# Batched matmul minus a tensor: the identity built on VectorE, and the first row tile cut as one block of 128 rows

## The chip, the cores and the metric

One Trainium2 chip, one of its cores. Times are device microseconds. Below 2% a difference counts as "same".

## The reference

```python
batch, m, k, n = 16, 512, 1024, 768          # all float32
out = np.matmul(x, weight) - sub_value        # x: (16, 512, 1024), weight: (1024, 768)
```

The 16 x 512 rows are taken as 8192 rows, in 64 tiles of 128 ("m tiles"). 25.2 MB of sub_value, 33.6 of x and 3.1 of weight come in, 25.2 MB go out.

## The kernel before

A row of m tiles is loaded as one transfer. `S = 8` says how rows are dealt: in a segment of 1024 rows, partition p holds the eight rows 8p to 8p+7, and tile j is the j-th row of every partition. So a transfer of eight tiles moves one piece of 32 KB (x) or 24 KB (sub_value, out) per partition, while tile 0 alone is 128 rows of 4 KB that lie 32 KB apart.

```python
S = 8
TRANSFERS = [('x', 0, 1), ('w', 0, 1), ('x', 1, 1), ('w', 1, 1), ('x', 2, 1), ('w', 2, 1),
    ('x', 3, 2), ('w', 3, 1), ('s', 0, 1), ('x', 5, 3), ('s', 1, 3), ('x', 8, 4), ...
    ('x', 24, 8), ('o', 0, 8), ('s', 24, 8), ('x', 32, 8), ...          # cut
    ('o', 56, 5), ('o', 61, 2), ('o', 63, 1)]                           # (kind, first tile, tiles)
x_s = x_flat.rearrange("(s p j) k -> s p j k", p=P, j=S)                # the same for sub_value and out
...
pool.add(lambda: nc.gpsimd.memset(idle_w, 0.0), then=count("idle"))     # operands of the warm-up matmuls
pool.add(lambda: nc.gpsimd.memset(idle_x, 0.0), then=count("idle"))
pool.add(lambda: nc.gpsimd.memset(ident, 0.0), then=count("ident"))
pool.add(lambda: nc.gpsimd.affine_select(out=ident, ..., fill=1.0), waits=[(counter["ident"], 1)], ...)
```

All transfers go out from SyncE's queue in the order of the list, each as soon as its buffer allows. ScalarE casts x to fp16, TensorE (for some tiles VectorE) transposes it with the identity, TensorE multiplies, VectorE subtracts in place and SyncE stores. TensorE starts with 14 idle matmuls. Before any work, TensorE, ScalarE and VectorE make a first pass over a branch:

```python
nc.regs_mov(turn, 0); nc.br("turn_head", ...)
# turn_head: turn == 0 -> "past", else -> "work";  past: turn += 1, back to turn_head while turn < 2
with nc.body("work", ...):
    act.emit(act.ops); dve.emit(dve.ops[:NEAR]); ...    # TensorE: a head, a loop of 10, a tail
```

## Time and profile before

| | before |
|---|---|
| time, median of 3 (range) | 210.98 us (210.87 to 211.11) |
| profiled span | 209.0 us |
| bytes moved, mean rate | 87.08 MB, 417 GB/s |
| TensorE busy / VectorE busy | 94% / 61% |
| x tile 0 landed, first and last DMA engine | 3.95 / 5.99 us |
| last matmul starts / last store landed | 201.75 / 207.75 us |

The lines that carry the argument are quoted in the prediction. One reading aid: a transfer is split over 16 DMA engines, and the trace holds one landing event per engine. A transfer is complete with the last of the 16: the cast of x tile 0 starts at 6.01 us, just after the last landing at 5.99. I quote the first, the 13th and the last in order of time (the records don't name the engine), since in this program one to three engines trail the rest, or the mean of the 16. Such landings, packet durations and the moments of single instructions are worked out from the trace's own records; the profile's tables don't print them.

### The profile page before, as it was taken

What the parts mean: (1) busy time and instruction counts of PE and PEld (TensorE: products, weight loads), DVE (VectorE), ACT (ScalarE), POOL (GpSimd) and SP (SyncE); (2) the same over time, 40 slices, a digit from 0 to 9 for tenths busy, and PEclk for the clock granted to TensorE, in tenths of its full rate; (3) what the DMA queues carried; (4) which work ended last, traced back from release to release, by engine and by line L of the source; (5) the groups of instructions that cost most, each with busy time, mean ns of one, the idle gap of its engine ahead of it and who ended that gap; (6) DMA issues with size and microseconds to landing.
All of it is one profiled execution on the core that took longest, in us unless ns stands there. A gap on an engine that the chain in (4) does not pass through costs nothing.

```text
span 209.0 us, 2630 instructions
## 1 busy us (share of the span) xinstructions
PE 196.5 (94%) x1234; PEld 75.5 (36%) x700; DVE 127.0 (61%) x216; ACT 109.0 (52%) x113; POOL 1.4 (1%) x9
## 2 busy tenths in 40 slices
PE   6998799979999999999999999999999999999960
PEld 0133334324434433433443443344344244334410
DVE  0132153975994795598299379569839938952330
ACT  2555559615772761945645576193564737507300
POOL 2000000000000000000000000000000000000000
PEclk9999999999999999999999999999999999999996
DMA  6999999999999999999999999999999999999993
GB/s 196 411 429 427 432 424 438 436 415 439 437 439 433 420 423 442 445 426 425 447 426 419 447 419 423 456 439 415 440 436 411 430 437 437 419 433 442 414 411 125
DMA packets 5476, 87.08 MB, mean 417 GB/s; under 512 B 608, under 2 KB 608, under 8 KB 1888
## 3 DMA queue, kind: packets, MB, share of 16 engines
q1 hardware_dynamic: 5472, 87.03, 97.7%
q14 instruction: 3, 0.02, 0.1%
q8 instruction: 1, 0.02, 0.0%
HBM read 61.87 MB, written 25.17 MB: 416 GB/s over the span
## 4 chain that ended last, share of the span: by engine, by line
PE 75%; DMA 12%; DVE 6%; SPq 3%; issue 1%; DVEq 0%
PE po_b L184 67%; DMA so_ring<-in_sub_value_dram 12%; PE pt_b L321 8%; DVE xtp_b L354 3%; DVE so_ring L403 2%; SPq L284 2%; SPq L248 1%; SPq L554 0%; DVEq L60 0%; SPq L134 0%
## 5 line engine op out<-in xcount | busy, mean ns | idle before, releaser
L184 PE MATMUL po_b<-w_sb,xt_b 128*128 128x384 f16 x704 | 126.0, 326 | 0.7 <-DVE w_sb L251 0.7
L403 DVE TENSOR_TENSOR so_ring<-po_b,so_ring 128x768 f32<-128x768 f32 x64 | 60.8, 957 | 58.2 <-PE po_b L184 40.9
L334 ACT COPY xt_b<-pt_b 128x1024 f16<-128x1024 f16 x44 | 44.5, 1012 | 67.2 <-PE pt_b L321 66.3
L354 DVE STREAM_TRANSPOSE xtp_b<-x16p_b 32x256 f32<-32x256 f32 x144 | 62.7, 435 | 2.4 <-ACT x16p_b L303 0.2
L184 PE MATMUL po_b<-w_sb,xtp_b 128*128 128x384 f16 x320 | 61.3, 326 | 1.2 <-DVE xtp_b L354 1.1
L383 PEld LDWEIGHTS <-xt_b 128*128 128x128 f16 x352 | 34.4, 98 | 58.4 <-issue 55.1
L303 ACT CAST x_b<-x_ring 128x1024 f16<-128x1024 f32 x46 | 47.2, 1048 | 4.5 <-DMA x_ring<-in_x_dram 4.5
L321 PE MATMUL pt_b<-ident,x_b 128*128 128x128 f32 x184 | 47.5, 274 | 1.6 <-ACT x_b L303 1.5
L321 PEld LDWEIGHTS pt_b<-ident,x_b 128*128 128x128 f32 x184 | 25.4, 141 | 45.8 <-issue 36.3
L303 ACT CAST x16p_b<-x_ring 128x1024 f16<-128x1024 f32 x18 | 18.8, 1046 | 13.0 <-DMA x_ring<-in_x_dram 13.0
L383 PEld LDWEIGHTS <-xtp_b 128*128 128x128 f16 x160 | 15.7, 98 | 19.8 <-issue 17.7
L251 DVE CAST w_sb<-so_ring 128x768 f16<-128x768 f32 x8 | 4.1, 557 | 15.5 <-DMA so_ring<-in_weight_dram 15.5
L184 PE MATMUL po_b<-idle_x,idle_w 128*128 128x512 f16 x26 | 9.0, 503 | 2.1 <-POOL idle_x L171 2.1
L334 ACT COPY xtp_b<-pt_b 128x1024 f16<-128x1024 f16 x2 | 2.0, 1012 | 2.5 <-PE pt_b L321 2.5
L303 ACT ACT_TABLE_LOAD x1 | 1.3, 1283 | 1.8 <-issue 1.8
L413 PEld LDWEIGHTS <-idle_w 128*128 128x128 f16 x4 | 0.4, 100 | 2.0 <-POOL idle_x L171 2.0
L171 POOL MEMSET idle_x<- 128x512 f16 x1 | 0.5, 530 | 0.0
L485 ACT CAST stub<-ident 128x1 f16<-128x1 f32 x2 | 0.4, 194 | 0.0
L173 POOL TENSOR_SCALAR_AFFINE_SELECT ident<-ident 128x128 f32<-128x128 f32 x1 | 0.3, 294 | 0.1
L462 POOL MEMSET mark<- 128x1 f32 x1 | 0.1, 99 | 24.6 <-ACT xtp_b L334 24.6
L170 POOL MEMSET idle_w<- 128x128 f16 x1 | 0.2, 205 | 0.5 <-SPq L134 0.5
L172 POOL MEMSET ident<- 128x128 f32 x1 | 0.2, 205 | 0.0
(4 smaller groups left out, 0.4 us busy)
## 6 DMA issues: line engine op xcount, KB each, us to landing
so_ring<-in_sub_value_dram SPq DMA_DIRECT2D x7, 3072.0 KB, 24.3
out_dram<-so_ring SPq DMA_DIRECT2D x7, 3072.0 KB, 25.9
x_ring<-in_x_dram SPq DMA_DIRECT2D x5, 4096.0 KB, 22.8
x_ring<-in_x_dram SPq DMA_DIRECT2D x2, 2048.0 KB, 26.5
so_ring<-in_weight_dram SPq DMA_DIRECT2D x4, 768.0 KB, 8.8
x_ring<-in_x_dram SPq DMA_DIRECT2D x1, 3072.0 KB, 28.0
x_ring<-in_x_dram SPq DMA_DIRECT2D x2, 1024.0 KB, 24.4
out_dram<-so_ring SPq DMA_DIRECT2D x1, 1920.0 KB, 10.2
```

Of the source, the lines that this page charges most:

```text
L171: pool.add(lambda: nc.gpsimd.memset(idle_x, 0.0), then=count("idle"))
L184: return nc.tensor.add_instruction(mybir.InstMatmult(name=nc.get_next_instruction_name(), engine=full.engine, ins=list(full.ins), outs=lis ...
L248: sp.add(lambda st=st, at=at: nc.sync.dma_start(out=st, in_=w_c[at]), then=(sem, 16))
L251: lambda at=at, r=r, st=st: nc.vector.tensor_copy(out=w_sb[:, at, r], in_=st[:, r]),
L284: sp.add(lambda here=here, there=there: nc.sync.dma_start(out=here, in_=there), waits, (sem, 16))
L303: act.add(lambda: nc.scalar.copy(out=to, in_=x_in), waits, count("cast"))
L321: pe.add(lambda: nc.tensor.transpose(words, from_, ident), waits, count("turn") if last else None)
L334: act.add(lambda: nc.scalar.copy(out=to, in_=pt_b[:, b]), waits, count("evac"))
L354: dve.add(lambda: nc.vector.transpose(xt[b * Q : (b + 1) * Q, :, a * Q : (a + 1) * Q], x16[a * Q : (a + 1) * Q, :, b * Q : (b + 1) * Q],), ...
L383: pe.add(lambda weights=weights: nc.tensor.ldweights(weights, tile_position=(0, 0)), [w for w in waits if w[0] in ready])
L403: dve.add(lambda: nc.vector.tensor_tensor(out=o, in0=po[:, :, :NS], in1=o, op=mybir.AluOpType.subtract), [landed["s", mi], (counter["mul"] ...
L413: pe.add(lambda: nc.tensor.ldweights(idle_w, tile_position=(0, 0)), [(counter["idle"], 2)])
```

## The change

Its intent: make tile 0 one compact block, so that the first load starts well, and build the identity on an engine that idles at the start. Its core:

```diff
-S = 8
+SEGMENTS = [(0, 1), (1, 7)] + [(at, 8) for at in range(8, 64, 8)]
-    ('x', 24, 8), ('o', 0, 8), ('s', 24, 8), ...
+    ('x', 24, 8), ('o', 0, 1), ('o', 1, 7), ('s', 24, 8), ...
+    def view(flat, at, n):
+        first, size = next(one for one in SEGMENTS if one[0] <= at < sum(one))
+        rows = flat[first * P : (first + size) * P].rearrange("(p j) c -> p j c", p=P, j=size)
+        return rows[:, at - first : at - first + n]
-    pool.add(lambda: nc.gpsimd.memset(ident, 0.0), then=count("ident"))
-    pool.add(lambda: nc.gpsimd.affine_select(out=ident, ...), ...)
+    dve.add(lambda: nc.vector.memset(ones, 1.0), then=count("ident"))           # 128x32
+    dve.add(lambda: nc.vector.memset(ident, 0.0), then=count("ident"))
+    dve.add(lambda: nc.vector.tensor_tensor_scan(out=along, data0=ones, data1=ones, ...), ...)
+    dve.add(lambda: nc.vector.transpose(across, along), ...)
+    for a in range(P // Q):                                                     # four 32x32 blocks
+        dve.add(lambda here=here: nc.vector.tensor_tensor(out=ident[here, here],
+            in0=along[here], in1=across[here], op=mybir.AluOpType.is_equal), ...)
```

## The prediction

> **What bounds the kernel now.** I read the page's slices first, then the chain that ended last, then the waits of TensorE, then busy time by stretch, then the first microseconds in order of time.
>
> The slices and the DMA summary come first:
>
> ```profile
> PE   6998799979999999999999999999999999999960
> DMA  6999999999999999999999999999999999999993
> GB/s 196 411 429 427 432 424 438 436 415 439 437 439 433 420 423 442 445 426 425 447 426 419 447 419 423 456 439 415 440 436 411 430 437 437 419 433 442 414 411 125
> ...
> q1 hardware_dynamic: 5472, 87.03, 97.7%
> ```
>
> Each digit is a fortieth of the 209.0 us span. The reader is to see that the DMA engines are full from the second slice to the last but one, at 410 to 456 GB/s, and that TensorE is full as well. The data queue alone holds the 16 engines for 97.7% of the span. So there are two bounds that nearly touch, and the question is which of them sets the end, and where there is air.
>
> ```profile
> by line: PE po_b L184 67.3%; DMA so_ring<-in_sub_value_dram 12.4%; PE pt_b L321 7.5%; DVE xtp_b L354 3.3%; DVE so_ring L403 2.2%; SPq L284 2.2%; SPq L248 1.3%; issue 0.6%; SPq L554 0.0%; DVEq L60 0.0%; SPq L134 0.0%
> ...
> 8.72 25.85 DMA so_ring<-in_sub_value_dram
> 34.66 1.82 DVE so_ring L403 x2
> 39.08 0.96 DVE so_ring L403
> 42.77 0.96 DVE so_ring L403
> 45.79 0.81 PE po_b L184 x4
> ```
>
> This is the chain of waits in order of time (start, length, what). Up to 34.57 us it is one load of sub_value, then VectorE, and from 45.79 us TensorE and nothing else until 202.1. The waits of TensorE say the same:
>
> ```profile
> PE pt_b L321 <- ACT x_b L303: 1.5, 1, 1.5
> PE po_b L184 <- DVE xtp_b L354: 1.1, 1, 1.1
> PE po_b L184 <- DVE w_sb L251: 0.7, 2, 0.5
> ```
>
> Everything TensorE waits for lies in the first 46 us, and all three go back to a landing (x, sub_value, weight). Busy time by stretch (columns: PE, PEld, DVE, ACT, POOL, clock, DMA share, GB/s):
>
> ```profile
> 2.00:3.00 1.00, 0.95 (x3) 0.10 (x1) 0.00 (x0) 1.00 (x1) 0.12 (x1) 1.00 0.91 168
> 3.00:4.00 1.00, 1.00 (x4) 0.00 (x0) 0.00 (x0) 0.06 (x1) 0.00 (x0) 1.00 1.01 383
> 4.00:6.00 2.00, 2.00 (x6) 0.00 (x0) 0.00 (x0) 0.00 (x0) 0.00 (x0) 1.00 0.98 382
> 46.00:100.00 54.00, 54.00 (x351) 21.71 (x201) 39.80 (x68) 30.12 (x31) 0.00 (x0) 1.00 1.01 433
> ```
>
> TensorE is busy 54.00 of 54 us in the middle, and the engines move 433 GB/s. From 2 to 6 us the engines are occupied but move less: that is the only stretch before the end where bytes are lost. Last, the start of the work:
>
> ```profile
> 1.82 0.29 POOL L173 TENSOR_SCALAR_AFFINE_SELECT ident<-ident 128x128 f32<-128x128 f32 x1
> 2.05 5.90 PE L184 MATMUL po_b<-idle_x,idle_w 128*128 128x512 f16 x14 [2.05 <-POOL idle_x L171]
> 6.01 1.05 ACT L303 CAST x_b<-x_ring 128x1024 f16<-128x1024 f32 x1 [2.95 <-DMA x_ring<-in_x_dram]
> 7.79 0.60 PE L321 MATMUL pt_b<-ident,x_b 128*128 128x128 f32 x4
> 7.90 1.03 DVE L251 CAST w_sb<-so_ring 128x768 f16<-128x768 f32 x2 [7.90 <-DMA so_ring<-in_weight_dram]
> ```
>
> The identity was ready at 2.1 us and first used at 7.6. x tile 0 was cast by 7.06, but TensorE was still in its 14 warm-up matmuls, so it began the transposes half a microsecond later.
>
> One thing the page doesn't show, from the trace's landing events (16 per transfer, one per DMA engine): x tile 0 landed at 3.95 us on the first engine and at 5.99 on the last; weight piece 1 at 9.13 and 11.02; sub_value tiles 4 to 7 at 32.71 and 34.57. The spread of 1.9 us is carried along unchanged. Its origin is in the packet records: two refills of instructions (8 KB, 1.65 us from 2.00; 16 KB, 0.93 us from 3.97) and data packets of 4 KB that took up to 1.10 us, against 0.159 us soon after. The last store, issued at 203.10, landed at 205.23 on the first engine and at 207.75 on the last. So the end is the slowest engine's queue, 2.5 us behind the fastest.
>
> **What the Trainium skill says.** "DMA: Bandwidth & Descriptors", section Queues, rings and completion order: each engine consumes its ring in order, and a transfer is complete only when all its engines have reported. The trace agrees: the lag of 1.9 us above never heals while the queues are full. The same page, section Where 436 GB/s comes from, gives 435 GB/s as the ceiling; the trace has 433 in the middle, so there is no rate left to gain there. Its section Latency and other measured facts warns of HBM row pitches at large powers of two, 512 KiB and up; the pitch here was 32 KiB and becomes 4 KiB (tile 0) and 28 KiB (tiles 1 to 7), and 4 KB packets already ran at 0.159 us, 25.8 GB/s per engine, so I see no aliasing to be cured. "VectorE: DVE Perf Modes", section The TRN2 errata, gives (N+151)/0.96 ns for an fp32 tensor_tensor; the trace's subtraction of 768 columns takes 957 ns, which is that formula's value.
>
> **The change part by part.**
>
> 1. The identity leaves GpSimd. Removed: a memset of 205 ns and a select of 294 ns, from 1.55 to 2.12 us, on an engine with nothing else to do. The warm-up tiles are written before them, so TensorE's start at 2.05 stays. Worth 0.
>
> 2. The identity comes to VectorE: two memsets, a scan, a transpose and four 32x32 comparisons. VectorE's branch into this code was at 1.99 us in the trace before. Estimate by the formula above: six operations of 32 columns at (32+151)/0.96 = 0.19 us make 1.14; the scan, if it costs twice per element, 0.22; the memset of 128 columns 0.29. Sum 1.66 us, so ready at about 3.7 us; even at twice that, 5.4. It is needed at 7.57, and VectorE's own next work is at 7.90. Worth 0.
>
> 3. The operations ahead move the point at which VectorE's program is cut by eight instructions. In the trace before, the transposes on both sides of the cut start 0.45 us apart like all others, so the cut costs nothing. Worth 0.
>
> 4. x tile 0 becomes one block of 512 KB instead of 128 rows 32 KB apart. Packets stay 4 KB per partition, so the steady rate is the same. What can improve is the slow beginning. Against 432 GB/s the stretches 2 to 3, 3 to 4 and 4 to 6 us lack 264, 49 and 100 KB, together 413 KB or 0.96 us of the stream. Most of that I take for the cold start of the engines and the instruction refills, which the change need not touch; I count a third of it, 0.3 us, as due to scattered rows. Since the queues never run dry, that third goes through to the end.
>
> 5. Tiles 1 to 7 and their sub_value and output: packets are the same but for the first store. 128 packets of 24 KB become 128 of 3 KB and 128 of 21 KB. A 3 KB packet took 121 ns in the trace, 40.3 ns per KB against 38.0 for a large one: 8 per engine lose 8 x 3 x 2.3 = 55 ns, and eight more packet starts are in that figure. One more issue by SyncE, some 0.43 us, on a queue that waits 84 us for casts anyway. Worth +0.05.
>
> Sum: 0 + 0 + 0 - 0.3 + 0.05, about -0.25; with some weight on the first rival below, -0.4. From 210.98 that is 210.6 us.
>
> **The rivals.** First: the change also removes or shifts an instruction refill at the start (GpSimd's program shrinks by the select and its set-up), so the slowest engine gains 0.7 to 1.6 us. For it: that engine's lag is visible from 5.99 us to the end, and the head of TensorE's chain hangs on it. Against: the records don't say whose instructions those are, and the select ran before the second refill began. It would make 209.5 to 210.2.
>
> Second: all is hidden. The warm-up matmuls end at 7.57 whatever x does, and the first weight piece lands at 7.87 behind x tile 0. Bytes in front are the same, so landings from weight piece 1 on don't move. For it: TensorE was already 0.5 us later than the cast. It would make 210.9 to 211.1.
>
> Third: a new cost. The identity is late, a split store delays the loads queued behind it, or a refill lands on an engine that is already last. For it: no slack in the DMA stream, so each lost 0.1 us of the slowest engine shows. Against: the terms above are small. It would make 211.1 to 211.6.
>
> **Range and chances.** The second rival and my sum share most of the weight, the first has about a quarter, the third a tenth. Three runs before span 210.87 to 211.11, so noise is 0.1. Hence 210.6, with 209.5 to 211.3 for eight times in ten. Two per cent is 4.2 us: to gain that, TensorE's unbroken 156 us after 45.79 would have to shrink, which no part touches, and to lose it an early wait would have to grow beyond all idle time seen. So 0.02, 0.96, 0.02.
>
> **What would show it right or wrong.** Right: the last VectorE operation on the identity ends before 5 us; the first transposes still start near 7.6 to 7.8; the GB/s of 2 to 4 us rise somewhat; sub_value tiles 4 to 7 land 0.2 to 0.5 us before 34.57; TensorE stays unbroken from about 45.5. For the first rival: the spread of the landings shrinks from 1.9 us, or a refill is gone from the packet records. For the second: the landings from weight piece 1 on stand where they stood. I'd be wrong outright if TensorE waited for the identity, if the packets of tiles 1 to 7 at 28 KB pitch took other than 0.159 us, or if the middle showed idle TensorE.

## The result

The changed kernel took 210.74 us in the median of four runs (210.42 to 211.31), the kernel before 211.05 (four runs). The ratio is 0.9991 with a 95% interval of 0.9975 to 1.0008. A ratio here is the mean time of one kernel's runs over the mean of the other's in the same rounds, so not quite the ratio of the medians.

Slices of the changed kernel:

```profile
DMA  6999999999999999999999999999999999999992
GB/s 198 412 425 436 435 426 437 447 434 429 419 464 437 382 417 447 447 414 440 445 419 419 451 437 395 481 419 417 470 412 430 403 442 451 433 400 447 431 398 116
...
q1 hardware_dynamic: 5616, 87.03, 97.6%
```

The queue is full as before. Slice 14 (about 68 to 73 us) is the lowest of the middle with 382 GB/s (420 before); slice 26 is down to 395 as well, so the slices alone prove nothing yet. The start of the changed kernel in order of time:

```profile
2.13 0.09 DVE L180 MEMSET ones<- 128x32 f32 x1 [2.13 <-issue]
2.19 0.17 DVE L181 MEMSET ident<- 128x128 f32 x1
2.27 0.20 DVE L182 TENSOR_TENSOR_SCAN along<-ones 128x32 f32<-128x32 f32 x1
2.51 0.21 DVE L185 STREAM_TRANSPOSE across<-along 128x32 f32<-128x32 f32 x1
2.75 0.83 DVE L188 TENSOR_TENSOR ident<-along,across 32x32 f32<-32x32 f32 x4
6.99 1.04 ACT L318 CAST x_b<-x_ring 128x1024 f16<-128x1024 f32 x1 [3.93 <-DMA x_ring<-in_x_dram]
8.08 0.66 PE L336 MATMUL pt_b<-ident,x_b 128*128 128x128 f32 x4 [0.32 <-ACT x_b L318]
```

The identity is complete at 3.58 us. But the first cast, at 6.01 before, now starts at 6.99, and this time TensorE waits for it, 0.32 us. Busy time by stretch in the changed kernel (columns as in the prediction; the last is GB/s):

```profile
2.00:3.00 1.00, 0.95 (x3) 0.10 (x1) 0.77 (x6) 1.00 (x1) 0.00 (x0) 1.00 0.88 233
3.00:4.00 1.00, 1.00 (x4) 0.00 (x0) 0.52 (x3) 0.06 (x1) 0.00 (x0) 1.00 1.04 404
4.00:6.00 2.00, 2.00 (x6) 0.00 (x0) 0.00 (x0) 0.00 (x0) 0.00 (x0) 1.00 0.96 338
```

From 2 to 4 us it moves 637 KB, against 551 before; from 4 to 6 us less than before, so that over 2 to 6 us the two are level (1313 and 1315 KB). The chain of waits in the changed kernel:

```profile
8.11 26.97 DMA so_ring<-in_sub_value_dram
35.16 1.82 DVE so_ring L418 x2
...
46.29 0.81 PE po_b L199 x4
```

The same chain, half a microsecond later (34.66 and 45.79 before). Sub_value tiles 4 to 7 landed at 32.37 us on the first engine, 32.92 on the 13th and 35.07 on the last (before: 32.71, 33.51, 34.57). So thirteen engines are earlier by 0.3 to 0.6 us and the last is later by 0.5. For the last one the packet records point to a refill of instructions (a packet of kind "instruction" in the page's list of queues) of 8 KB that took 1.58 us from 2.70 us, and to refills of 8 and 16 KB at 3.72 and 3.78. Before they stood at 2.00 (1.65 us), 3.97 and 3.97. That a refill is the cause is tested below (`no_first_pass`).

My theory at this point (A): scattered rows slowed the first packets, the new rows cure that, but the engine that a refill holds hides it. Rivals: the identity on VectorE made the better start (B); all of it is the scatter of single executions (C). Twelve runs followed: ten edited kernels, and each of the two kernels once more.

### The profile page after: what moved, and what is told of

It reads as the page before. It is cut to its first block, busy times and chain, and to the rows that moved or that the text cites. A ratio compares the mean times of both kernels' runs of the same rounds, so it can differ in the third digit from the quotient of the medians.

```text
span 209.0 us, 2635 instructions
## 1 busy us (share of the span) xinstructions
PE 196.4 (94%) x1234; PEld 75.4 (36%) x700; DVE 128.2 (61%) x224; ACT 109.0 (52%) x113; POOL 1.0 (0%) x7
## 4 chain that ended last, share of the span: by engine, by line
PE 75%; DMA 13%; DVE 6%; SPq 3%; issue 1%; DVEq 0%
PE po_b L199 67%; DMA so_ring<-in_sub_value_dram 13%; PE pt_b L336 8%; DVE xtp_b L369 3%; DVE so_ring L418 2%; SPq L299 2%; SPq L263 1%; SPq L569 0%; DVEq L60 0%; SPq L139 0%
## 5 line engine op out<-in xcount | busy, mean ns | idle before, releaser
L188 DVE TENSOR_TENSOR ident<-along,across 32x32 f32<-32x32 f32 x4 | 0.7, 183 | 0.1
```

What stands on the lines that cost most here:

```text
L188: dve.add(lambda here=here: nc.vector.tensor_tensor(out=ident[here, here], in0=along[here], in1=across[here], op=mybir.AluOpType.is_equal, ...
```

## The experiments

Each was run beside the kernel before, on the same chip. The median of before was not the same in each of the four calls below: 210.90, 211.12, 211.26 and 211.17 us. So only ratios are compared across calls, which ran on three chips. All runs were fast, except that the one run of `before_again` (210.89 us) has an unknown state; only its profile is used. Each profile is one execution.

### The two halves apart, and repeats

`rows_only` is the changed kernel with the identity back on GpSimd; `ident_only` has the identity on VectorE and the old rows.

```diff
 # rows_only, against the changed kernel
-    dve.add(...memset ones / memset ident / scan / transpose / 4 x is_equal...)
+    pool.add(lambda: nc.gpsimd.memset(ident, 0.0), ...); pool.add(lambda: nc.gpsimd.affine_select(...), ...)
 # ident_only, against the changed kernel
-SEGMENTS = [(0, 1), (1, 7)] + [(at, 8) for at in range(8, 64, 8)]
+SEGMENTS = [(at, 8) for at in range(0, 64, 8)]
-('o', 0, 1), ('o', 1, 7),
+('o', 0, 8),
```

> Only the row layout changes; the identity stays on GpSimd. Theory A (scattered rows slowed the first packets): the stretch 2 to 3 us moves about 230 GB/s as in the changed kernel, not 168, and the first 12 or 13 of the 16 landings of weight piece 1 come by about 9.7 us, the last of sub_value tiles 4 to 7 is still decided by one engine that an instruction refill held; the time is 0.0 to 0.3 us below before. Theory B (the identity on VectorE made the better start): 168 GB/s and landings as in the kernel before. Theory C (the difference is the scatter of single executions): neither can be told from a repeat of before.

> Only the identity moves to VectorE; rows as before. Theory A: 2 to 3 us moves about 170 GB/s, landings of weight piece 1 between 9.1 and 10.0 us on the first 13 engines, time equal to before within 0.1 us. Theory B: about 230 GB/s and a time 0.2 to 0.3 us below before. Identity complete at about 3.6 us in both.

The two kernels once more, unedited, for second profiles:

> The kernel before, once more, for a second profile. Theory A: 2 to 3 us again moves 160 to 180 GB/s. Theory C: it differs from 168 by as much as the changed kernel's 233 does, or the last landing of sub_value tiles 4 to 7 wanders by 0.5 us (34.57 before, 35.07 in the changed kernel).

> The changed kernel, once more. Theory A: 2 to 3 us again moves 220 to 240 GB/s, ratio to before 0.998 to 1.000. Theory C: the GB/s or the last landings wander as much as the two kernels differ, and the ratio's interval includes 1.

The stretch from 2 to 3 us, first in `rows_only`, then in `ident_only`, then in the repeat of before, then in the repeat of the changed kernel:

```profile
2.00:3.00 1.00, 0.95 (x3) 0.10 (x1) 0.00 (x0) 1.00 (x1) 0.11 (x1) 1.00 0.83 266
```

```profile
2.00:3.00 1.00, 0.95 (x3) 0.10 (x1) 0.77 (x6) 1.00 (x1) 0.00 (x0) 1.00 0.89 164
```

```profile
2.00:3.00 1.00, 0.95 (x3) 0.10 (x1) 0.00 (x0) 1.00 (x1) 0.11 (x1) 1.00 0.89 168
```

```profile
2.00:3.00 1.00, 0.95 (x3) 0.11 (x1) 0.76 (x6) 1.00 (x1) 0.00 (x0) 1.00 0.99 315
```

Old rows give 168, 168 and 164 GB/s, new rows 233, 266 and 315. A gives the right order and B falls. But the two executions of the changed kernel lie 82 GB/s apart, more than the 65 between the first pair, and outside the 220 to 240 that I expected. What carries A is that the two sets don't overlap, also with the runs that follow: 164 to 176 in four profiles with rows 32 KB apart, 229 to 315 in six with the new rows. Nor is it the moment of the first refill: that stood at 2.66 to 2.72 us in the three profiles here with new rows, but at 2.04 to 2.08 in `load_rows`, `store_swapped` and `store_later`, which moved 250, 258 and 229 GB/s. Of the landings C is partly right: the last engine's landing of sub_value tiles 4 to 7 came at 34.57 and 35.07 in two executions of before, and at 35.07 and 34.12 in two of the changed kernel. It wanders by as much as the 13th engine gained, or more. (In `rows_only` the 13th landing of weight piece 1 came at 9.96 us and not by 9.7, so it shows no gain there.)

The times: `rows_only` 210.68 us (ratio 0.9991, interval 0.9979 to 1.0003), `ident_only` 210.54 (0.9981, 0.9966 to 0.9996), the changed kernel 210.85 (0.9997, 0.9980 to 1.0013). The half without the better start has the lowest ratio, and its interval ends just below 1, which theory A did not foresee. But the changed kernel holds the same edit and stands at 0.9997, so I don't count it as a gain of that half.

One more thing came out of the repeats. In all six profiles so far the last store landed between 207.55 and 207.79 us, although TensorE's last matmul started anywhere from 201.29 to 202.25. And between 62 and 82 us the three profiles with the new rows lost time: from the full landing of sub_value tiles 16 to 23 to that of output tiles 0 to 7 took 17.0 us three times with old rows, and 17.5, 18.2 and 17.9 with the new. That stretch contains the divided first store.

### Is it the divided store?

`load_rows` keeps the new rows for x and sub_value but stores tiles 0 to 7 undivided to the old places (a wrong result). `split_store` is the kernel before with only the store divided. `store_swapped` is the changed kernel with tiles 1 to 7 stored first.

```diff
 # load_rows, against the changed kernel
-('o', 0, 1), ('o', 1, 7),
+('o', 0, 8),
-        first, size = next(one for one in SEGMENTS if ...)
+        first, size = (at // 8 * 8, 8) if kind == 'o' else next(one for one in SEGMENTS if ...)
 # split_store, against the kernel before
-('o', 0, 8),
+('o', 0, 1), ('o', 1, 7),
 # store_swapped, against the changed kernel
-('o', 0, 1), ('o', 1, 7),
+('o', 1, 7), ('o', 0, 1),
```

> The changed kernel with the first store undivided, 24 KB per partition to the old places (wrong result on purpose: tiles 0 to 7 come out with permuted rows). Theory D (the divided store with 3 KB rows gives back what the start gains): 2 to 3 us still moves 230 to 315 GB/s; between the full landing of sub_value tiles 16 to 23 and that of output tiles 0 to 7 lie 17.0 us, as in the kernel before, not the 17.5 to 18.2 of the kernels with the new rows; the last landing of the program moves from 207.7 to about 207.2 and the time to about 210.3 (ratio 0.997). Theory E (the end is pinned by something else, the start doesn't matter): the last landing stays at 207.6 to 207.8 and the ratio at 0.999 to 1.000.

> The kernel before with its first store divided into tile 0 and tiles 1 to 7, rows as before. Theory D: the 17.0 us between those two landings become 17.4 to 18.2, and the time rises by 0.3 to 0.8 us (ratio 1.001 to 1.004). Theory E: 17.0 to 17.1 us and a ratio within 0.001 of 1.

> The changed kernel with the store of tiles 1 to 7 ahead of that of tile 0, so the short rows follow a store and not a load. Theory D1 (the loss is in the step from a load of 32 KB rows to a store of 3 KB rows): 17.0 to 17.2 us between the two landings, the time about 210.3. Theory D2 (the loss is in short store rows wherever they stand): 17.5 us or more again, time as the changed kernel's 210.7 to 210.9.

`load_rows`: 210.67 us, ratio 0.9979 (0.9959 to 1.0000). Those two landings were 17.9 us apart (63.02 and 80.92) although the store was whole. `split_store`: 211.07 us, ratio 0.9998 (0.9978 to 1.0018), and 17.15 us apart although the store was divided. Theory D, that the divided store gives the start's gain back, fell from both sides. Theory E is nearer, though the last store of `load_rows` landed at 207.46 and its ratio is 0.9979, both a little below E's range. `store_swapped`: 210.89 us, 0.9985 (0.9963 to 1.0008), 17.0 us apart; but its engines were held in this execution, with 14 packets of 4 or 6 KB stretched that start between 8 and 10.5 us, so it came to 62 us without a lead and decides nothing about the order of the stores.

Looking at single packets showed what the lost time is. In the changed kernel, 14 packets of 32 KB took 1.37 to 2.05 us instead of 1.21, starting at 68.5 to 70.2 us; 13 of them overlap in time, so they probably ran on as many engines. They belong to the load of x tiles 24 to 31, just ahead of the first store. In windows, first the kernel before, then the changed kernel, then `load_rows`:

```profile
66.00:70.00 4.00, 4.00 (x29) 1.82 (x17) 1.66 (x2) 3.44 (x4) 0.00 (x0) 1.00 0.97 418
70.00:74.00 4.00, 4.00 (x29) 1.75 (x16) 3.89 (x9) 2.44 (x3) 0.00 (x0) 1.00 0.95 408
```

```profile
66.00:70.00 4.00, 4.00 (x28) 1.78 (x16) 1.16 (x2) 2.94 (x4) 0.00 (x0) 1.00 1.18 483
70.00:74.00 4.00, 4.00 (x29) 1.69 (x16) 3.92 (x8) 2.92 (x3) 0.00 (x0) 1.00 0.88 364
```

```profile
66.00:70.00 4.00, 4.00 (x28) 1.86 (x17) 1.91 (x4) 3.87 (x5) 0.00 (x0) 1.00 1.19 483
70.00:74.00 4.00, 4.00 (x28) 1.73 (x16) 3.88 (x8) 1.76 (x2) 0.00 (x0) 1.00 0.84 356
```

The stretched packets are booked by their start, so the first window shows a share over 1 and the second a hole: 364 and 356 GB/s, where before has 408. Because of this booking the two windows together show no loss (424, 420 and 413 GB/s in the changed kernel, `load_rows` and before). The landings do. By the mean of the 16, x tiles 24 to 31 landed 9.68 to 9.73 us after sub_value tiles 16 to 23 in the nine profiles without stretching at that load, and 10.04, 10.47, 10.04, 10.00 and 10.34 in the changed kernel, its repeat, `rows_only`, `load_rows` and (below) `no_first_pass`. The excess over 9.71 is, within 0.03 us, the stretched time divided by 16 (0.31, 0.78, 0.35, 0.30 and 0.60; the sums are in the table below). So the stretching accounts for the lead that is lost there. TensorE is at 4.00 of 4 us throughout and doesn't wait.

### Does the distance between rows matter at all?

`pitch_256k` is the kernel before with one segment of 64 tiles: the same packets, but the rows of one tile 256 KB apart.

```diff
-S = 8
+S = 64
```

> The kernel before with one segment of 64 tiles, so the rows of one tile lie 256 KB apart (output correct, packets of the same sizes). Theory A (distance between rows slows the start): 2 to 3 us moves less than the 168 GB/s of 32 KB apart, perhaps 120, and x tile 0 lands on the first 14 engines later than 4.5 us. If only the cold start counts: 165 GB/s again. If such a distance hurts in the steady state as well, 46 to 200 us moves below 425 GB/s and the time rises by several per cent.

211.35 us, ratio 1.0014 (0.9987 to 1.0041). It moved 213 and 250 GB/s in the third and fourth microsecond, 463 KB together. Set beside the others, 2 to 4 us moved 463 KB at 256 KB between rows; 514 to 553 at 32 KB (`split_store` 514; before, its repeat and `ident_only` 549 to 553); 637 to 690 with tile 0 as one block, 4 KB between rows (both of the changed kernel, `rows_only`, `load_rows`, `store_swapped`, `store_later`). The microsecond from 2 to 3 us went the wrong way (213, above 168); the two together go in order. By 6 us the order is gone between 256 and 32 KB: from 2 to 6 us 1267 KB against 1263 to 1315, while the new rows have 1313 to 1398. From 46 to 200 us `pitch_256k` ran at 430 to 433 GB/s like the rest. So a compact tile 0 starts better than scattered rows; that a wider scatter costs more isn't shown by this one profile.

### When does the loss near 70 us appear, and what do the refills cost?

`store_later` moves the sub_value load of tiles 24 to 31 ahead of the first stores. `no_first_pass` takes the first pass over the branch away, in the hope of taking the refills at 2 to 4 us with it.

```diff
 # store_later, against the changed kernel
-('o', 0, 1), ('o', 1, 7), ('s', 24, 8), ('x', 32, 8),
+('s', 24, 8), ('o', 0, 1), ('o', 1, 7), ('x', 32, 8),
 # no_first_pass, against the changed kernel
-    turn = nc.alloc_registers("turn", ...) ... the branch, "work", "past", "rest"
+    act.emit(act.ops); dve.emit(dve.ops); pe.emit(head); pe.emit_loop(...); pe.emit(tail)
```

> The changed kernel with the load of sub_value tiles 24 to 31 moved ahead of the first stores. In all four kernels with the new rows whose start was quick, packets of the load ahead of the first store (x tiles 24 to 31) were stretched at about 69.5 to 70.2 us, together 5.5 to 13 us over 16 engines, and no store began before 71.1 us. Theory F (the step from the load to the first store holds the engines): no packet of 32 KB near 70 us is stretched, the stretch moves to the end of the sub_value load near 78 us or is gone. Theory G (a moment of time near 70 us, whatever is in the queue): the packets near 70 us are stretched as before, by 5 us or more in sum. Time 210.3 to 210.9 either way.

> The changed kernel without the first pass over its branch, so TensorE, ScalarE and VectorE run straight into their work. Theory H (the instruction refills at 2 to 5 us, which put one to three DMA engines 1 to 2 us behind for the whole run, come from that pass, and they set the end): the refills of 8 KB between 2 and 4 us are gone or fewer, the spread of the 16 landings of sub_value tiles 4 to 7 falls from 1.5 to 2.7 us to under 1 us, and the time falls to 209.5 to 210.3, unless refills later in the run take their place. If the refills belong to something else: they stand, with a spread of 1.5 us or more, and the time stays within 0.3 us of 210.8.

`store_later`: 210.65 us, ratio 0.9972 (0.9957 to 0.9987). No packet near 70 us was stretched; 12 packets of 24 KB were, starting at 76.4 to 78.0, in the sub_value load that now stands just ahead of the first store. So the loss goes with the step from loads to the first store (F), not with a moment (G). At the later steps from loads to stores no profile has a like group of stretched packets.

`no_first_pass`: 210.75 us, ratio 0.9977 (0.9962 to 0.9992). The refills at the start are gone, and the start is what one would wish for:

```profile
1.67 4.97 PE L199 MATMUL po_b<-idle_x,idle_w 128*128 128x512 f16 x14 [1.67 <-POOL idle_x L179]
4.44 1.04 ACT L318 CAST x_b<-x_ring 128x1024 f16<-128x1024 f32 x1 [2.25 <-DMA x_ring<-in_x_dram]
6.47 0.60 PE L336 MATMUL pt_b<-ident,x_b 128*128 128x128 f32 x4
```

Cast at 4.44 instead of 6.99, first transposes at 6.47 instead of 8.08. The 16 landings of sub_value tiles 4 to 7 lie within 0.43 us (32.29 to 32.72) instead of 2.7. Yet the last store landed at 207.41 us, against 207.75. The lead of 2.3 us on the last engine went in two visible steps. A refill of 16 KB came at 35.2 us and took 0.93 us, and the spread at the next landing is 1.8 us again (37.12 to 38.89). Then 24 packets near 70 us were stretched by 9.6 us in sum, the second largest amount of all. More refills came at 50.3, 87.3 and 145.2 us. TensorE ended 1.4 us earlier than in the changed kernel (last subtraction at 201.21 instead of 202.61) and waited for the last stores the longer:

```profile
203.00:205.00 2.00, 0.00 (x0) 0.00 (x0) 0.00 (x0) 0.00 (x0) 0.00 (x0) 0.57 0.95 392
205.00:207.00 2.00, 0.00 (x0) 0.00 (x0) 0.00 (x0) 0.00 (x0) 0.00 (x0) 0.50 0.16 65
```

Here, at the end of `no_first_pass`, TensorE is at 0.00 and the engines still move 392 GB/s; after 205 us only a few of them are left. Theory H was right that the pass brings the early refills, and that these make the spread of the early landings; but removing them brought the last store forward by 0.34 us only, and the time not to the 209.5 to 210.3 that it expected. Since later refills took their place, a run without any refill stays untested.

### The kernel before without the pass, and everything together

```diff
 # before_no_first_pass: the kernel before with the edit of no_first_pass
 # all_together: the changed kernel with the edits of no_first_pass and store_later
```

> The kernel before (old rows, identity on GpSimd) without the first pass over the branch. The refills at 2 to 4 us should be gone as in the changed kernel without that pass, and sub_value tiles 4 to 7 land fully by about 33.7 us. Theory L (the loads ahead of the first store are slowed whenever the queue is early, whatever the rows): sub_value tiles 16 to 23 land on the first engine at about 61.9 us, little or no stretching near 70 us (under 2 us in sum), and the program's last landing comes at 206.8 to 207.3. Theory R (only the new rows have it): no stretching at all. If stretching of 5 us or more shows with the first landing at 61.9 or later, what the quick runs share is that the engines run in step, not that they are early.

> The changed kernel without the first pass and with the sub_value load of tiles 24 to 31 ahead of the first stores: the two edits that came out lowest. If their gains add, ratio 0.994 to 0.996 and about 209.9 to 210.3 us; if the loads ahead of the first store give the lead back again, some 5 to 11 us of stretching in sum near 76 to 78 us and a ratio of 0.997 to 0.998, no lower than each alone.

`before_no_first_pass`: 210.87 us, ratio 0.9990 (0.9977 to 1.0003). Sub_value tiles 16 to 23 landed on the first engine at 61.86 us, nothing near 70 us was stretched, and the last store landed at 207.41, a little later than expected. So did the last of tiles 4 to 7 (34.34, not 33.7), after a refill of 16 KB at 30.5 us that took 1.08. L and R both foretold the absence of stretching, so it doesn't part them. `all_together`: 210.97 us, ratio 0.9992 (0.9978 to 1.0005), with 21 packets stretched by 6.9 us in sum ahead of the first store. The two edits don't add. So the ratios of 0.997 to 0.998 that `store_later`, `no_first_pass` and `ident_only` showed alone can't be relied on: none of these versions is clearly better than both kernels.

The fourteen profiles in one table, ordered by the first landing of sub_value tiles 16 to 23 (us; "stretched" is the time by which packets between 66 and 79 us exceeded the median of their size, summed over those that exceeded it by more than 0.15 us):

| profile | tiles 4-7: 13th / last | tiles 16-23: first | stretched | last matmul starts | last store landed | ratio |
|---|---|---|---|---|---|---|
| after_again | 32.81 / 34.12 | 61.33 | 12.5 | 201.29 | 207.74 | 0.9997 |
| no_first_pass | 32.54 / 32.72 | 61.38 | 9.6 | 200.84 | 207.41 | 0.9977 |
| all_together | 32.72 / 34.20 | 61.39 | 6.9 | 201.38 | 207.86 | 0.9992 |
| rows_only | 33.19 / 34.45 | 61.45 | 5.6 | 201.62 | 207.55 | 0.9991 |
| changed kernel | 32.92 / 35.07 | 61.52 | 5.0 | 202.25 | 207.75 | 0.9991 |
| load_rows | 32.84 / 33.90 | 61.52 | 4.8 | 201.07 | 207.46 | 0.9979 |
| store_later | 33.20 / 34.80 | 61.63 | 3.3 | 201.97 | 207.57 | 0.9972 |
| ident_only | 33.28 / 34.95 | 61.69 | 0.5 | 202.12 | 207.63 | 0.9981 |
| before_no_first_pass | 33.36 / 34.34 | 61.86 | 0.0 | 201.52 | 207.41 | 0.9990 |
| split_store | 33.50 / 34.37 | 61.97 | 0.2 | 201.55 | 207.88 | 0.9998 |
| before | 33.51 / 34.57 | 62.01 | 0.0 | 201.75 | 207.75 | |
| pitch_256k | 33.47 / 35.09 | 62.09 | 0.0 | 202.26 | 208.06 | 1.0014 |
| store_swapped | 34.33 / 35.59 | 62.11 | 0.0 | 202.76 | 208.13 | 0.9985 |
| before_again | 33.59 / 35.07 | 62.28 | 0.0 | 202.24 | 207.79 | |

The order is striking: the earlier the queue, the more of it is stretched away ahead of the first store, and from 61.69 us on next to nothing is. The last landing of tiles 4 to 7 covers 2.9 us, the last store 0.7.

What stays open: why loads slow down ahead of the first store in the early runs. All seven of them also load by the new rows. The new rows alone don't do it: `store_swapped` has them too, came late by accident (first landing at 62.11), and had nothing stretched, though the two parts of its first store stand in the other order. Whether earliness alone does it is open: a kernel with old rows that is as early would tell. And past 82 us the slowest engine goes its own way: from there to the last store took 126.1 to 127.1 us in the profiles that keep the order of the list. I can name late refills as one part of it, not the whole.

## Why the prediction was right

**The bound.** Right. (The section that the prediction cites for 435 GB/s has that figure for the ports of the on-chip memory, and names about 358 for transfers with HBM; the 430 to 433 measured here decide that.) Both bounds were there, and the slowest engine's queue sets the end: in `no_first_pass` TensorE ended 1.4 us earlier than in the changed kernel, and the last store landed only 0.34 us earlier. TensorE stayed unbroken from 46.29 us in the changed kernel (45.5 foretold), and the packets of 4 KB kept their 0.159 us.

**Term 1, the identity leaves GpSimd: 0.** Right. The warm-up matmuls start at 2.05 us in both kernels.

**Term 2, the identity on VectorE: 0, ready at about 3.7 us.** Right: complete at 3.58. The comparisons took 180 to 189 ns each (0.19 foretold), the scan 202 (0.22), the transpose 211 (0.19), the memset of 128 columns 165 (0.29) and that of 32 columns 85 (0.19).

**Term 3, the cut moved by eight instructions: 0.** Right: the transpose behind the cut starts 0.45 us after the one ahead of it (124.95 and 124.50 us), like any other. What did move is a later refill: at 160.9 to 162.7 us in the profiles with the identity on GpSimd, at 143.2 to 145.8 with it on VectorE. It took about 0.3 us on one engine, early or late.

**Term 4, the compact tile 0: -0.3 us, "that third goes through to the end".** The first half holds in direction: 2 to 4 us moved 637 to 690 KB instead of 514 to 553, and the 13th engine landed tiles 4 to 7 about 0.5 us earlier: at 32.97 in the mean of three profiles (the changed kernel, its repeat, `rows_only`) against 33.46 in that of three others (before, its repeat, `ident_only`). But less than half of that lead was there at the end of the cold start. By the mean of the 16 landings, the profiles with new rows (without `store_swapped` and the two that lack the first pass) had weight piece 1 at 9.44 to 9.65 us against 9.69 to 9.81 with rows 32 KB apart, some 0.2 us, and sub_value tiles 16 to 23 at 61.83 to 62.09 against 62.32 to 62.77, some 0.6. So most was won between 10 and 62 us, where the prediction had "the steady rate is the same". Packets of 12 KB took 0.460 us in the median of the run in all eight profiles with the new rows and 0.465 in four of the six with the old. `ident_only` and `before_again` had 0.460 with the old rows, so the rows alone don't explain it, and the cause is open. The second half is the step that failed. The gain wasn't carried to the end: the last stores landed at 207.75, 207.74 and 207.55 us against 207.75, 207.79 and 207.63. Over all profiles that keep the first pass it was 207.70 us in the mean with the new rows (six) and 207.82 with the old (five), less apart than single executions are. I had argued that the queues never run dry and that a lead therefore persists. They never ran dry, but that isn't enough. The end hangs on the slowest engine, which refills of up to 2.5 us hold back, and packets were stretched ahead of the first store, by 5.0 us in sum or 0.31 per engine in the changed kernel, while every engine counted as busy.

**Term 5, the divided store: +0.05 us.** Right by the packets: 0.121 + 0.799 us took the place of 0.912, eight times per engine, which makes 0.06 us. The ratio with it alone, 0.9998 (0.9978 to 1.0018), is too coarse to show so little.

**The rivals.** The first (a refill removed) didn't happen: the refills stood with the identity on either engine. (In before there were three at the start, not two as I had read; a second one of 8 KB took 0.31 us from 3.97.) Had it happened, it would have been worth less than the 0.7 to 1.6 us that I gave it: with the early refills gone altogether, the ratio was 0.9977, and 0.9990 and 0.9992 in two other kernels, though later refills took their place. The second (all hidden) is nearest to the outcome if one goes by the ratio (0.9991 of 210.98 is 210.8), but not by its mechanism: landings from weight piece 1 on did move, on thirteen engines. The signs that I had named for my sum came out mixed: more bytes early, yes; tiles 4 to 7 landing fully 0.2 to 0.5 us sooner, no (0.5 later in one execution, 0.45 sooner in the other); first transposes near 7.6 to 7.8, no (8.08, because the refill had delayed x tile 0's last landing to 6.96).

So 210.6 us and its range of 209.5 to 211.3 held the measured 210.74, and "within 2%" was safe since the unbroken TensorE stretch left nothing larger to win. But the -0.4 in it was not shown: the measured ratio's interval contains 1, and the repeat gave 0.9997. That 210.6 came so close to 210.74 is luck.

## What to carry to other kernels

When one transfer is split over 16 engines, ask where the last of the 16 stands, and take two profiles before believing a shift of half a microsecond in it. A gain at the head of a saturated queue is real only if it is still there at the last store: follow it landing by landing, for it may be handed back by other traffic or by slower packets, with no engine ever idle. And when two bounds nearly touch, speeding up one alone can be worth nothing, as in `no_first_pass`, where TensorE ended 1.4 us earlier.

## What the Trainium skill lacked or had wrong

- "DMA: Bandwidth & Descriptors", section Latency and other measured facts, lists losses from the distance between rows from 512 KiB on. Below that the steady rate was indeed untouched (430 to 433 GB/s at 256 KB), but in the first microseconds a compact tile 0 did better: 637 to 690 KB from 2 to 4 us with tile 0 as one block, 514 to 553 at 32 KB between rows, 463 at 256 KB; from 2 to 6 us 1313 to 1398, 1263 to 1315 and 1267. The page has nothing on how the distance between rows bears on the first microseconds.
- "Runtime: NRT & Kernel Launch", section Instruction fetch mechanics, has refills in blocks of 16 KiB and calls their cost mostly hidden. In these runs they came as packets of 8 KB and one of 16 KB per run. At the start they took up to 2.5 us, and at sub_value tiles 4 to 7 one engine stood up to 2.7 us behind the first; without them it was 0.43 (`no_first_pass`). The section's warning that a branch breaks prefetch fits: without the first pass, the refills at 2 to 4 us were gone, and others came at 29.6 to 35.2 us and later.
- No page has the stretching of loads ahead of the first store: 12 to 24 packets over by 3.3 to 12.5 us in sum in the seven earliest profiles, none to two in the others.
- "VectorE: DVE Perf Modes", section The TRN2 errata: (N+151)/0.96 ns for tensor_tensor came within 6% also at N = 32 (191 by it, 180 to 189 measured for a comparison). For a memset of 128 fp32 columns it isn't meant, and gave too much (290 against 165).
